# Storing the split weights of a four-chunk decoder block, a fifth place for them, and gates of 64 rows

## The chip, the core and the metric

One core of a Trainium2 chip runs the kernel in one launch. The metric is the device time of an execution in microseconds. The core's engines run beside each other and each takes its own instructions in order: TensorE (PE) multiplies, VectorE (DVE) and ScalarE (ACT) do element-wise work, SyncE (SP) issues nearly all DMA transfers, GpSimd (POOL) has almost nothing here. A DMA that SP issues may wait for a semaphore first; what is behind it in SP's program waits with it.

## What is computed

A decoder block of width 1024 over 2048 positions with 16 learned ones in front, in fp32. Cut to what matters:

```python
u = rmsnorm(h, mix_norm_g)
p = u @ w_in                                  # "W": 1024 x 1792
y = concat(pool(p_a), conformer(p_b), rglru(p_c))
h = h + y @ w_out                             # "O": 1024 x 1024
u = rmsnorm(h, mlp_norm_g)
h = h + square(relu(u @ w_up)) @ w_down       # "U" 1024 x 4096, "D" 4096 x 1024
out = rmsnorm(h, final_norm_g)[:, 16:]
# in rglru: 8 heads of 64 channels, two gates
r = sigmoid(einsum("bthc,hcd->bthd", xh, w_a) + b_a)
i = sigmoid(einsum("bthc,hcd->bthd", xh, w_x) + b_x)
```

## The kernel before

**Arithmetic.** Each fp32 operand of a product is held as a pair hi and lo: `split` (L109 to L111) rounds the source to hi with an ACT copy (L110) and takes lo as the rest with a DVE subtraction (L111). A product is three matmuls, hi·hi, hi·lo and lo·hi (`PRODS`), added in a PSUM bank.

**Tiling.** Channels lie on the 128 partitions, positions along the free axis, in four chunks of 512 columns; chunk 0 has the 16 learned positions besides, and its subtiles outside of O, U and D are 264 columns wide. A weight tile of 128x512 holds four 128-channel blocks of the contraction for one block of 128 output channels. For W, O and D an output tile (`mm_tile`) takes two weight tiles, each in 12 matmuls of 512 columns (L278; D's first two tiles of a group are interleaved, L292). In chunks 1 to 3 the up product U is a Strassen-Winograd scheme: 16 units of seven weight tiles, each tile in 12 matmuls of 256 columns (`up_unit`, L302). Of the seven, three are plain weights and four are sums and differences of weights, which chunk 0 works out (`gen_sums`) and leaves in the DRAM tensor `sums`.

**Order of the items.** W for chunks 0 and 1 interleaved, O for chunk 0, the rest of W for chunk 1; then for each chunk four groups of U and D. Behind the last D of chunk 0 stand O of chunk 1 and W of chunk 2, behind that of chunk 1 O of chunk 2 and W of chunk 3; O of chunk 3 stands within the last D group of chunk 2. O(c) and W(c) below are these products for chunk c, with tiles 0 to 7 of O and 0 to 13 of W.

**Weights.** The class `Weights` is one stream over all weight tiles in the order of use. `dma` loads a raw tile of 256 KB into one of six places `wr` (L141, on SP). `split` turns it into a tile `wh` of hi and lo, 128x1024, of which there are `WH` = 4 places; it does so under `tc.high_priority(EARLY)`, so the scheduler puts the two split instructions ahead of other work. A raw load waits until the split (L111) of an earlier tile has freed its place; a split waits until PE has read the `wh` tile that was in its place.

**Around O.** While PE runs O(c), ACT and DVE do two other things that load rows of the input through the two places `xr`. The evacuation `evac_o` of tile j loads the residual (L713), adds it to the PSUM tile into `h` (L715) and sums the squares of h (L345, L346). PE can't start a tile before the add of four tiles earlier has freed its PSUM bank (`pm` has four). And `gen_x` for chunk c+1 loads its eight input blocks (L412), sums their squares (L345, L346) and makes the pairs `U` that W will read (L148, L149). Both end in a `colsum` (L327, L328), two matmuls with a matrix of ones over the summed squares, then a square root (L335) and a reciprocal (L337). The scheduler lays the instructions of each engine in one list; waits and order are fixed when the program is built.

**Gates.** `gen_rg` takes a 128-channel block, that is two heads. `c_gw` holds block-diagonal 128x128 matrices, so each gate is three matmuls of 128 rows (`mm3`, L311 to L313) into a bank of `pb` (two banks) and one sigmoid of 128 partitions (L580).

## Time and profile before

| | |
|---|---|
| median of 3 runs | 1967.27 us (1966.43 to 1970.16) |
| the profiled execution | 1964.15 us, of which the span is 1962.2 us; granted clock 0.998 |
| PE busy | 1932.9 us, 99% of the span |
| DVE, ACT busy | 1508.6 us (77%), 1097.9 us (56%) |
| moved by DMA | 285.07 MB, 145 GB/s in the mean |

In the profile an instruction is named by its line, engine, operation and the tiles it writes and reads. "Idle before" is the time in which the engine stood before an instruction of the group, with what ended it. A row of the timeline gives the start, the length, and with "x24" a run of 24 like instructions; on SPq the length is that of issuing the transfers. The matmul's end is modelled: a matmul of 512 columns shows some 395 ns from start to end, but in a run of them the next starts long before that.

### The profile page before, as it was taken

Reading aid. Unit: us, or ns where it says so; the run is one execution under the profiler, and the core shown is the slowest. Engines: PE = TensorE matmul, PEld = TensorE weight load, DVE = VectorE, ACT = ScalarE, POOL = GpSimd, SP = SyncE. Lnnn points to the kernel's source line nnn. Section 1 sums busy time; section 2 is a strip of 40 time slices with the busy share of each in tenths; the row PEclk is TensorE's granted clock in tenths of the full one; section 3 lists DMA queues with packets and bytes.
Section 4 is the critical chain, followed back from the end, with each engine's and each line's share of the span. In section 5 each row is a group of like instructions: output and inputs, shape, how many; then the busy total and the mean of one; then the engine's idle time right before and its main releaser. Section 6 shows DMA issues by size and latency. Waiting matters only on the chain.

```text
span 1962.2 us, 29710 instructions
## 1 busy us (share of the span) xinstructions
PE 1932.9 (99%) x10648; PEld 1664.7 (85%) x10648; DVE 1508.6 (77%) x2419; ACT 1097.9 (56%) x1837; POOL 0.2 (0%) x4
## 2 busy tenths in 40 slices
PE   8999999999999999999999999999999999999998
PEld 8888878878888789898898778988989889889897
DVE  7986689977756899985776799986768597656477
ACT  6575463646544536675575453775658356445374
POOL 0000000000000000000000000000000000000000
PEclk9999999999999999999999999999999999999999
DMA  6412456645755435353444543544435434545354
GB/s 199 135 44 76 129 169 218 212 159 171 267 174 162 144 92 168 90 166 108 146 133 125 184 127 108 151 115 141 139 117 163 132 103 151 170 137 151 113 173 150
DMA packets 160035, 285.07 MB, mean 145 GB/s; under 512 B 17552, under 2 KB 23824, under 8 KB 159888
## 3 DMA queue, kind: packets, MB, share of 16 engines
q1 hardware_dynamic: 158304, 281.55, 46.6%
q8 instruction: 83, 1.36, 0.3%
q10 hardware_dynamic: 1584, 1.64, 0.2%
q14 instruction: 64, 0.52, 0.1%
HBM read 255.85 MB, written 27.26 MB: 144 GB/s over the span
## 4 chain that ended last, share of the span: by engine, by line
PE 77%; DVE 11%; DMA 6%; issue 3%; ACT 3%; SPq 1%; ACTq 0%; DVEq 0%
PE pm L278 47%; PE pm L302 11%; PE pw L302 9%; PE pm L292 7%; DVE wh L111 3%; DMA s<-d_w_up 2%; DMA xr<-d_xr 2%; DVE ca L535 1%; DMA t<-d_w_up 1%; DVE t L569 1%; DVE fr L821 1%; ACT wh L110 1%; DVE U L795 0%; DMA sums<-s 0%; PE pb L311 0%
## 5 line engine op out<-in xcount | busy, mean ns | idle before, releaser
L110 ACT ACTIVATE wh<-wr 128x512 fp32r<-128x512 f32 x828 | 517.1, 627 | 710.4 <-PE pm L278 482.9
L278 PE MATMUL pm<-U,wh 128*128 128x512 f32 (+1 forms) x3504 | 788.2, 384 | 0.6 <-DVE wh L111 0.6
L278 PEld LDWEIGHTS pm<-U,wh 128*128 128x128 f32 x3504 | 635.2, 188 | 141.0 <-DVE wh L111 1.0
L111 DVE TENSOR_TENSOR wh<-wr,wh 128x512 fp32r<-128x512 f32 x828 | 567.4, 689 | 208.6 <-ACT wh L110 204.1
L278 PE MATMUL pm<-H,wh 128*128 128x512 f32 (+1 forms) x2112 | 450.2, 372 | 8.0 <-ACT wh L110 6.5
L278 PEld LDWEIGHTS pm<-H,wh 128*128 128x128 f32 x2112 | 370.6, 190 | 82.9 <-ACT wh L110 6.5
L302 PE MATMUL pm<-H,wh 128*128 128x256 f32 x2304 | 292.5, 282 | 2.3 <-DVE wh L111 1.4
L302 PEld LDWEIGHTS pm<-H,wh 128*128 128x128 f32 x2304 | 282.3, 188 | 5.2 <-DVE wh L111 2.2
L302 PE MATMUL pw<-H,wh 128*128 128x256 f32 x1728 | 223.2, 282 | 1.6 <-DVE fr L821 1.6
L302 PEld LDWEIGHTS pw<-H,wh 128*128 128x128 f32 x1728 | 212.0, 189 | 4.6 <-DVE fr L821 3.9
L292 PE MATMUL pm<-U,wh 128*128 128x512 f32 (+1 forms) x768 | 176.1, 388 | 0.0
L292 PEld LDWEIGHTS pm<-U,wh 128*128 128x128 f32 x768 | 140.2, 188 | 30.9 <-DVE U L795 0.2
L535 DVE SCALAR_TENSOR_TENSOR ca<-Pbv,vec,ca 128x512 f32<-128x512 f32 x180 | 128.1, 748 | 0.0
L850 DVE TENSOR_TENSOR h<-h,pm 128x512 f32<-128x512 f32 (+1 forms) x106 | 71.6, 675 | 60.5 <-PE pm L278 45.6
L795 DVE TENSOR_TENSOR U<-fr,U 128x512 fp32r<-128x512 f32 x128 | 87.6, 687 | 11.4 <-ACT fr L794 11.4
L793 ACT ACTIVATE U<-fr 128x512 fp32r<-128x512 f32 x128 | 79.6, 624 | 1.9
L794 ACT ACTIVATE fr<-fr 128x512 f32<-128x512 f32 x128 | 79.3, 622 | 1.1
L821 DVE TENSOR_TENSOR fr<-pw,fr 128x512 f32<-128x512 f32 x96 | 66.1, 689 | 4.5 <-PE pw L302 1.9
L346 DVE TENSOR_TENSOR ss<-ss,fr 128x512 f32<-128x512 f32 (+1 forms) x82 | 53.3, 650 | 15.9 <-ACT fr L345 15.3
L337 DVE RECIPROCAL rs<-rs 128x512 f32<-128x512 f32 (+2 forms) x17 | 53.9, 3169 | 10.8 <-ACT rs L335 10.6
L535 DVE SCALAR_TENSOR_TENSOR ca<-h,vec,ca 128x512 f32<-128x512 f32 x60 | 42.8, 748 | 0.1
L841 ACT ACTIVATE fr<-fr 128x512 f32<-128x512 f32 x48 | 30.0, 625 | 12.1 <-DVE fr L840 11.8
(211 smaller groups left out, 1153.0 us busy)
## 6 DMA issues: line engine op xcount, KB each, us to landing
wr<-d_w_down SPq DMA_DIRECT2D x272, 256.0 KB, 2.9
wr<-d_w_up SPq DMA_DIRECT2D x208, 256.0 KB, 2.9
wr<-sums SPq DMA_DIRECT2D x192, 256.0 KB, 3.3
wr<-d_w_in SPq DMA_DIRECT2D x90, 256.0 KB, 2.7
xr<-d_xr SPq DMA_DIRECT2D x56, 256.0 KB, 2.8
wr<-wo_fold SPq DMA_DIRECT2D x32, 256.0 KB, 2.6
wr<-d_w_out SPq DMA_DIRECT2D x32, 256.0 KB, 2.6
s<-d_w_up SPq DMA_DIRECT2D x32, 256.0 KB, 3.8
```

The lines of the kernel that those rows point to most:

```text
L110: A.activation(out=hi, in_=src, func=AF.Copy)
L111: V.tensor_tensor(out=lo, in0=src, in1=hi.bitcast(F32), op=ALU.subtract)
L278: T.matmul(ps[:, : s1 - s0], w[k // 4][:, a, (k % 4) * P : (k % 4 + 1) * P], rhs[k][:, b, s0:s1], start=(k == 0 and j == 0), stop=(k == KB ...
L292: T.matmul(ps[:, : s1 - s0], w[k // 4][:, a, (k % 4) * P : (k % 4 + 1) * P], rhs[k][:, b, s0:s1], start=(k == 0 and j == 0), stop=(k == KB ...
L302: T.matmul(ps, w[:, a, k * P : (k + 1) * P], op[k // 2][:, b, (k % 2) * 256 : (k % 2) * 256 + 256], start=(k == 0 and j == 0), stop=(k == ...
L337: V.reciprocal(rs[:, c0:c1], rs[:, c0:c1])
L535: V.scalar_tensor_tensor(out=a, in0=o.ub[i][:, k : k + NT], scalar=vc("cw", i * CONVK + k), in1=a, op0=ALU.mult, op1=ALU.add)
L793: A.activation(out=f[:, 0], in_=r, func=AF.Square)
L794: A.activation(out=r, in_=r, func=AF.Square)
L795: V.tensor_tensor(out=f[:, 1], in0=r, in1=f[:, 0].bitcast(F32), op=ALU.subtract)
L821: V.tensor_tensor(out=out.rearrange("p (a c) -> p a c", a=2), in0=ps.rearrange("p (a c) -> p a c", a=2), in1=x.unsqueeze(1).broadcast_to([ ...
L850: V.tensor_tensor(out=h, in0=h, in1=ps[:, : s1 - s0], op=ALU.add)
```

## The change

Each split weight tile of W, of O and of the four sums of a U unit is written to DRAM once and loaded again as a pair. New DRAM tensors `w_kept` (28 tiles), `o_kept` (16) and `u_kept` (64), 512 KB each, take the `wh` tile behind its first split: W and O in the first use (28 and 16 stores), the sums in chunk 1 (64 stores). Where a tile has been kept, `split` issues one DMA from it into `wh` on SP (L271 in the new numbering), within the same `tc.high_priority(EARLY)`, in place of the raw load, the ACT copy and the DVE subtraction: 64 loads for W(2), W(3) and what W(1) takes again, 48 for O(1) to O(3), 128 for the sums in chunks 2 and 3. `WH` goes from 4 to 5, and with it the lookahead of the stream. In the gates `c_gw` becomes 128x512: rows 0 to 63 hold the even head's matrices, rows 64 to 127 the odd head's. A gate pair is now six matmuls of 64 rows each, alternating between the low and the high half and between two banks, and four sigmoids of 64 partitions (120 such matmuls in 25 runs over the program; before, 120 matmuls of 128 rows).

```diff
@@ -43,7 +43,7 @@
 HB = 14
 NU = D * 4 // (2 * P)
 WR = 6
-WH = 4
+WH = 5
 FR = 4
 LA_SPLIT = WH
 EARLY = 200
...
@@ -133,6 +133,9 @@
     cst = {}
 
     wo_fold = dp.tile([KB, P, 512], F32, name="wo_fold", tag="wo_fold")
+    w_kept = [[dp.tile([P, 2, 512], F32, name=f"wk_{b}_{q}", tag=f"wk_{b}_{q}") for q in range(2)] for b in range(14)]
+    o_kept = [[dp.tile([P, 2, 512], F32, name=f"ok_{j}_{q}", tag=f"ok_{j}_{q}") for q in range(2)] for j in range(KB)]
+    u_kept = [[dp.tile([P, 2, 512], F32, name=f"uk_{u}_{q}", tag=f"uk_{u}_{q}") for q in range(4)] for u in range(NU)]
     sums = [dp.tile([P, 2048], F32, name=f"sums_{u}", tag=f"sums_{u}") for u in range(NU)]
 
     def w_raw(src, tag="xr", bufs=2, queue=nc.sync):
...
@@ -205,9 +208,8 @@
         yield 1400
 
     def load_consts():
-        hl = t_("c_gw", (2, 1024), 1, F32R)
-        for c0 in (0, 512):
-            split(hl[:, 0, c0 : c0 + 512], hl[:, 1, c0 : c0 + 512], w_raw(gates[:, c0 : c0 + 512]))
+        hl = t_("c_gw", (2, 512), 1, F32R)
+        split(hl[:, 0], hl[:, 1], w_raw(gates))
         cst["gw"] = hl
         yield 1500
 
...
@@ -242,6 +244,8 @@
 
 
     class Weights:
+
+
         def __init__(self, srcs):
             self.srcs = srcs
             self.raw = {}
...
@@ -251,15 +255,24 @@
 
         def dma(self, n):
             while self.nd < min(n, len(self.srcs)):
-                self.raw[self.nd] = w_raw(self.srcs[self.nd](), "wr", WR, nc.sync if self.nd > 1 else nc.scalar)
+                if self.srcs[self.nd][2] is not None:
+                    self.nd += 1
+                    continue
+                self.raw[self.nd] = w_raw(self.srcs[self.nd][0](), "wr", WR, nc.sync if self.nd > 1 else nc.scalar)
                 self.nd += 1
 
         def split(self, n):
             while self.ns < min(n, len(self.srcs)):
                 self.dma(self.ns + 1)
                 t = t_("wh", (2, 512), WH, F32R)
+                _, keep, kept = self.srcs[self.ns]
                 with tc.high_priority(EARLY):
-                    split(t[:, 0], t[:, 1], self.raw.pop(self.ns))
+                    if kept is not None:
+                        nc.sync.dma_start(out=t.bitcast(F32), in_=kept)
+                    else:
+                        split(t[:, 0], t[:, 1], self.raw.pop(self.ns))
+                if keep is not None:
+                    nc.sync.dma_start(out=keep, in_=t.bitcast(F32))
                 self.hl[self.ns] = t
                 self.ns += 1
 
...
@@ -572,12 +585,18 @@
         w = cst["gw"]
         r = t_("t", W0, TB)
         g = t_("t", W0, TB)
-        for q, (dst, bias) in enumerate(((r, "ba"), (g, "bx"))):
-            for s0, s1 in subs_of(o):
-                ps = ps_back()
-                o_ = q * 512 + i * P
-                mm3(ps[:, : s1 - s0], [(w[:, 0, o_ : o_ + P], w[:, 1, o_ : o_ + P], hi[:, s0:s1], lo[:, s0:s1])])
-                A.activation(out=dst[:, s0:s1], in_=ps[:, : s1 - s0], func=AF.Sigmoid, bias=vc(bias, i))
+
+        low, high = slice(0, 64), slice(64, P)
+        for s0, s1 in subs_of(o):
+            n = s1 - s0
+            pa, pb_ = ps_back(), ps_back()
+            for j, (a, b) in enumerate(PRODS):
+                for ps, h in ((pa, low), (pb_, high)):
+                    T.matmul(ps[:, :n], w[h, a, i * P : (i + 1) * P], (hi, lo)[b][h, s0:s1], start=(j == 0), stop=(j == 2))
+            for dst, ps, to, of, bias in (
+                (r, pa, low, low, "ba"), (r, pb_, high, high, "ba"), (g, pa, low, high, "bxs"), (g, pb_, high, low, "bxs"),
+            ):
+                A.activation(out=dst[to, s0:s1], in_=ps[of, :n], func=AF.Sigmoid, bias=vc(bias, i)[of])
         yield 620
         csp = cst["csp"]
         a = t_("t", W0, TB)
...
@@ -951,31 +970,42 @@
         kind, c, j, _ = it
         if kind == "U" and c:
             m1, m2, s = w_up[2 * j], w_up[2 * j + 1], sums[j]
-            aps = (
-                (m1, 0), (m1, 512), (s, 0), (s, 1536), (s, 1024), (s, 512), (m2, 512),
-            )
-            return ("U", j), [lambda a=a, c0=c0: a[:, c0 : c0 + 512] for a, c0 in aps]
+            aps = [(m1, 0), (m1, 512), (s, 0), (s, 1536), (s, 1024), (s, 512), (m2, 512)]
+            r = []
+            for a, c0 in aps:
+                kept = u_kept[j][c0 // 512] if a is s else None
+                if kept is not None and c > 1:
+                    r.append((None, None, kept))
+                else:
+                    r.append((lambda a=a, c0=c0: a[:, c0 : c0 + 512], kept, None))
+            return r
+        keep = (None, None)
         if kind == "W":
-            a = w_in[_WORDER[j][2]]
+            b = _WORDER[j][2]
+            if c > 1 or ("W", b) in seen:
+                return [(None, None, t) for t in w_kept[b]]
+            a, keep = w_in[b], w_kept[b]
         elif kind == "U":
             a = w_up[j]
         elif kind == "D":
             a = w_down[j // KB, j % KB]
         else:
-            return ("O", j), [lambda: wo_fold[j], lambda: w_out[j]]
-        return (kind, a.offset if hasattr(a, "offset") else j, j), [lambda a=a, c0=c0: a[:, c0 : c0 + 512] for c0 in (0, 512)]
-
-    srcs, windex, last = [], [], None
+            if c:
+                return [(None, None, t) for t in o_kept[j]]
+            return [(lambda: wo_fold[j], o_kept[j][0], None), (lambda: w_out[j], o_kept[j][1], None)]
+        return [(lambda a=a, c0=c0: a[:, c0 : c0 + 512], keep[c0 // 512], None) for c0 in (0, 512)]
+
+    srcs, windex, last, seen = [], [], None, set()
     for it in items:
-        key, aps = sources(it)
-        if it[0] == "U":
-            key = ("U", it[1] > 0, it[2])
-        if it[0] == "W":
-            key = ("W", _WORDER[it[2]][2])
+        kind, c, j, _ = it
+        key = (kind, j if kind != "W" else _WORDER[j][2])
+        if kind == "U":
+            key += (c,)
         if key != last:
             first = len(srcs)
-            srcs.extend(aps)
+            srcs.extend(sources(it))
             last = key
+            seen.add(key)
         windex.append(first)
     wts = Weights(srcs)
 
...
@@ -1091,13 +1121,16 @@
...
-        "bx": _chan(a["rg_b_x"][0]), "rcb": _chan(a["rg_conv_b"][0]), "cb": _chan(a["convb_dw_b"][0]),
+        "bxs": np.roll(_chan(a["rg_b_x"][0]), 64, axis=0), "rcb": _chan(a["rg_conv_b"][0]), "cb": _chan(a["convb_dw_b"][0]),
...
-    gates = np.concatenate([_blockdiag(a["rg_w_a"][0]), _blockdiag(a["rg_w_x"][0])], axis=1).reshape(P, 1024)
+    gates = np.concatenate([
+        np.concatenate([a["rg_w_a"][0][0::2], a["rg_w_x"][0][0::2]], axis=2),
+        np.concatenate([a["rg_w_x"][0][1::2], a["rg_w_a"][0][1::2]], axis=2),
+    ], axis=1).transpose(1, 0, 2).reshape(P, 512)
```

**SP in O(2).** Before, from the second block of `gen_x`'s loads that are still out to the residual of tile 3: `wr` are raw weight loads, `xr` at L412 the input blocks for chunk 3, `xr_1758` and `xr_1778` at L713 the residuals of tiles 2 and 3.

```order
L412 DMA xr_1751_10348<-d_xr 128x512 [waits DMAHW5_49,DMAHW3_49,DVE_49]
L713 DMA xr_1758_10390<-d_xr 128x512 [waits DMAHW6_49,DMAHW4_49,DVE_49]
L141 DMA wr_1787_10488<-d_w_in 128x512 [waits DVE_49]
L141 DMA wr_1794_10528<-d_w_in 128x512 [waits DVE_49]
L412 DMA xr_1762_10398<-d_xr 128x512 [waits DMAHW7_49,DMAHW3_49,DVE_49]
L412 DMA xr_1765_10406<-d_xr 128x512 [waits DMAHW4_49,DMAHW0_49,DVE_49]
L141 DMA wr_1795_10530<-d_w_in 128x512 [waits DMAHW1_49,DVE_49]
L412 DMA xr_1768_10414<-d_xr 128x512 [waits DMAHW7_49,DMAHW2_49,DVE_49]
L141 DMA wr_1802_10570<-d_w_in 128x512 [waits DVE_49]
L412 DMA xr_1771_10422<-d_xr 128x512 [waits DMAHW0_49,DVE_49]
L141 DMA wr_1803_10572<-d_w_in 128x512 [waits DMAHW5_49,DVE_49]
L713 DMA xr_1778_10464<-d_xr 128x512 [waits DMAHW6_49,DMAHW2_49,DVE_49]
```

Now, the same place (L425 is L412 of before, L732 is L713): `wh` are loads of kept pairs, each waiting for PE; `ok_7_0` and `ok_7_1` are the two weight tiles of O's tile 7, `wk_2_0`, `wk_2_1` and `wk_4_0` the first ones of W(3); `xr_1692` and `xr_1710` are the residuals of tiles 2 and 3.

```order
L425 DMA xr_1684_10400<-d_xr 128x512 [waits DMAHW1_49,DVE_49]
L271 DMA wh_1728_10600<-ok_7_1_119 128x1024 [waits DMAHW2_49,PE_49]
L425 DMA xr_1687_10408<-d_xr 128x512 [waits DMAHW7_49,DMAHW3_49,DVE_49]
L271 DMA wh_1729_10602<-wk_2_0_80 128x1024 [waits DMAHW4_49,PE_49]
L732 DMA xr_1692_10444<-d_xr 128x512 [waits DMAHW5_49,DMAHW1_49,DVE_49]
L425 DMA xr_1696_10452<-d_xr 128x512 [waits DMAHW6_49,DMAHW3_49,DVE_49]
L425 DMA xr_1699_10460<-d_xr 128x512 [waits DMAHW5_49,DVE_49]
L425 DMA xr_1702_10468<-d_xr 128x512 [waits DMAHW6_49,DMAHW0_49,DVE_49]
L425 DMA xr_1705_10476<-d_xr 128x512 [waits DMAHW7_49,DVE_49]
L271 DMA wh_1734_10636<-wk_2_1_81 128x1024 [waits DMAHW2_49,PE_49]
L271 DMA wh_1735_10638<-wk_4_0_84 128x1024 [waits PE_49]
L732 DMA xr_1710_10512<-d_xr 128x512 [waits DMAHW4_49,DMAHW0_49,DVE_49]
```

The loads of `xr` stood between raw loads that waited for DVE; they now stand behind loads that wait for PE to be done with the weight tile five places back: for `wh_1728` the first half of tile 5, for `wh_1729` its second half, for `wh_1734` and `wh_1735` the two halves of tile 6.

**DVE at the end of O(2).** Before: `hl_1781` is the low half for the column sum, `h_1779` tile 3, `h_1790` tile 4.

```order
L346 TENSOR_TENSOR ss_1741_10324<-ss_1741_10324,fr_1772_10424 128x512 [waits DVE_49,Activation_49]
L149 SCALAR_TENSOR_TENSOR U_1770_10421<-xr_1771_10422,vec_1_69,U_1770_10421 128x512 [waits DMAHW4_49,Activation_49]
L111 TENSOR_TENSOR hl_1781_10471<-ss_1741_10324,hl_1781_10471 128x512 [waits Activation_49]
L715 TENSOR_TENSOR h_1779_10466<-pm_1777_10439,xr_1778_10464 128x512 [waits DMAHW6_49]
L111 TENSOR_TENSOR wh_1809_10609<-wr_1787_10488,wh_1809_10609 128x512 [waits DMAHW5_49,Activation_49]
L337 RECIPROCAL rs_1783_10477<-rs_1783_10477 128x512 [waits Activation_49]
L111 TENSOR_TENSOR wh_1835_10681<-wr_1794_10528,wh_1835_10681 128x512 [waits Activation_49]
L346 TENSOR_TENSOR ss_1730_10260<-ss_1730_10260,fr_1780_10468 128x512
L715 TENSOR_TENSOR h_1790_10517<-pm_1788_10490,xr_1789_10515 128x512 [waits DMAHW0_49]
```

Now: `hl_1713` is that low half, `h_1711` tile 3, `h_1720` tile 4 (L734 is L715 of before, L350 is L337).

```order
L359 TENSOR_TENSOR ss_1677_10384<-ss_1677_10384,fr_1706_10478 128x512 [waits DVE_49,Activation_49]
L152 SCALAR_TENSOR_TENSOR U_1704_10475<-xr_1705_10476,vec_1_69,U_1704_10475 128x512 [waits DMAHW1_49,Activation_49]
L111 TENSOR_TENSOR hl_1713_10519<-ss_1677_10384,hl_1713_10519 128x512 [waits Activation_49]
L350 RECIPROCAL rs_1715_10525<-rs_1715_10525 128x512 [waits Activation_49]
L734 TENSOR_TENSOR h_1711_10514<-pm_1709_10487,xr_1710_10512 128x512 [waits DMAHW4_49,PE_49]
L734 TENSOR_TENSOR h_1720_10559<-pm_1718_10532,xr_1719_10557 128x512 [waits DMAHW5_49,PE_49]
L359 TENSOR_TENSOR ss_1668_10326<-ss_1668_10326,fr_1712_10516 128x512 [waits Activation_49]
L359 TENSOR_TENSOR ss_1668_10326<-ss_1668_10326,fr_1721_10561 128x512 [waits DVE_49,Activation_49]
```

The add of tile 3 stood ahead of the reciprocal and now stands behind it.

**PE in the gates of chunk 1.** Before, one block's two gates, with the matmuls of W around them:

```order
L278 MATMUL pm_508_2969<-U_466_2740,wh_500_2922 128x512 x3
L311 MATMUL pb_512_3000<-hl_509_2995,c_gw_97_504 128x512
L312 MATMUL pb_512_3000<-hl_509_2995,c_gw_97_504 128x512 [waits DVE_49]
L313 MATMUL pb_512_3000<-hl_509_2995,c_gw_97_504 128x512
L311 MATMUL pb_513_3005<-hl_509_2995,c_gw_97_504 128x512
L312 MATMUL pb_513_3005<-hl_509_2995,c_gw_97_504 128x512
L313 MATMUL pb_513_3005<-hl_509_2995,c_gw_97_504 128x512
L278 MATMUL pm_519_3028<-U_395_2360,wh_504_2959 128x512 [waits Activation_49]
```

Now (L595 is the new matmul, L291 is L278 of before):

```order
L291 MATMUL pm_501_3114<-U_459_2885,wh_492_3064 128x512 x3
L595 MATMUL pb_505_3145<-hl_502_3140,c_gw_99_628 128x512
L595 MATMUL pb_506_3146<-hl_502_3140,c_gw_99_628 128x512
L595 MATMUL pb_505_3145<-hl_502_3140,c_gw_99_628 128x512 [waits DVE_49]
L595 MATMUL pb_506_3146<-hl_502_3140,c_gw_99_628 128x512
L595 MATMUL pb_505_3145<-hl_502_3140,c_gw_99_628 128x512
L595 MATMUL pb_506_3146<-hl_502_3140,c_gw_99_628 128x512
L291 MATMUL pm_512_3175<-U_388_2505,wh_493_3067 128x512 [waits Activation_49]
```

Six matmuls in three and three became six in alternation between two banks; their number is the same.

More of the change, by code (lines that the diff above doesn't have):

```diff
@@ L60 @@
 _VECS = [
-    ("g1", 8), ("g2", 8), ("gf", 8), ("psc", 2), ("lam", 4), ("ba", 4), ("bx", 4),
+    ("g1", 8), ("g2", 8), ("gf", 8), ("psc", 2), ("lam", 4), ("ba", 4), ("bxs", 4),
     ("rcb", 4), ("cb", 2), ("lng", 2), ("lnb", 2), ("rcw", 16), ("cw", 62),
@@ L1112 @@
     "x0": (KB, P, W0), "xr": (NCH - 1, KB, P, NT), "w_in": (14, P, D), "w_out": (KB, P, 512), "w_fold": (4, P, D), "w_up": (32, P, D),
-    "w_down": (FG, KB, P, D), "vecs": (P, NVEC), "gates": (P, 1024), "pools": (P, 256), "pws": (P, 512),
+    "w_down": (FG, KB, P, D), "vecs": (P, NVEC), "gates": (P, 512), "pools": (P, 256), "pws": (P, 512),
 }
```

## The prediction

> **What bounds the kernel.** I read the busy times first, then the busy time in six stretches, then the waits of PE.
>
> ```profile
> PE 1932.9 (99%) x10648; PEld 1664.7 (85%) x10648; DVE 1508.6 (77%) x2419; ACT 1097.9 (56%) x1837; POOL 0.2 (0%) x4
> 0.00:130.00 130.00, 120.75 (x741) 107.78 (x742) 115.91 (x226) 83.21 (x126) 0.20 (x4) 1.00 0.43 136
> 130.00:600.00 470.00, 467.08 (x2015) 376.42 (x2013) 352.08 (x547) 257.76 (x417) 0.00 (x0) 1.00 0.53 168
> 600.00:1100.00 500.00, 495.12 (x2764) 428.08 (x2763) 395.41 (x627) 285.36 (x477) 0.00 (x0) 1.00 0.44 133
> 1100.00:1200.00 100.00, 98.70 (x420) 78.37 (x420) 90.42 (x146) 49.90 (x83) 0.00 (x0) 1.00 0.48 152
> 1200.00:1600.00 400.00, 398.82 (x2363) 351.33 (x2362) 308.49 (x484) 235.34 (x398) 0.00 (x0) 1.00 0.44 132
> 1600.00:1962.00 362.00, 352.45 (x2353) 322.67 (x2351) 246.31 (x394) 186.36 (x336) 0.00 (x0) 0.99 0.49 148
> PE pm L278 <- ACT wh L110: 6.5, 1, 6.5
> 1953.30 0.70 PE L865 MATMUL pb<-fr,ones 128*128 128x256 f32 x2 [0.59 <-ACT fr L856]
> ```
>
> A stretch's row gives its length, then PE, PEld, DVE, ACT and POOL busy, the granted clock, the share of DMA time and GB/s. PE is idle for 9.2, 2.9, 4.9, 1.3, 1.2 and 9.6 us, 29.1 in all. The first wait of the program is 6.5 of them, and 8.2 lie behind the last matmul, which ends at 1954.0 of 1962.2. **So some 14 us are all that a better supply of weights can win**; the rest is PE's own work. That work is paced by the start of the next matmul:
>
> ```profile
> 632.64 15.95 PE L278 MATMUL pm<-H,wh 128*128 128x512 f32 x68
> 844.58 3.03 PE L302 MATMUL pm<-H,wh 128*128 128x256 f32 x24
> L278 PE MATMUL pm<-H,wh 128*128 128x512 f32 x1632 | 384.1, 395 | 0.8 <-DVE h L715 0.5 <-DVE wh L111 0.2
> ```
>
> 68 matmuls of 512 columns take 15.95 us with the last one's 0.395: 0.232 us apart. 24 of 256 columns, by the same reckoning with 0.28, 0.119 apart. A weight tile of W, O or D is 12 x 0.232 = 2.8 us of PE, an O tile 5.6; a U tile 1.43, a unit of seven 10.0.
>
> **What the change takes away.**
>
> ```profile
> L110 ACT ACTIVATE wh<-wr 128x512 fp32r<-128x512 f32 x828 | 517.1, 627 | 710.4 <-PE pm L278 482.9
> L111 DVE TENSOR_TENSOR wh<-wr,wh 128x512 fp32r<-128x512 f32 x828 | 567.4, 689 | 208.6 <-ACT wh L110 204.1
> SPq L141 <- DVE wh L111: 1276.6, 741, 10.1
> ```
>
> 240 splits go: 240 x 0.627 = 150 us of ACT and 240 x 0.689 = 165 us of DVE. All of it ran beside PE: ACT's copies waited 483 us for PE, so they were early. It gains nothing beyond the 14 us. The third row is the side effect: SP's raw loads waited for the DVE split, 741 times. A kept load waits for PE instead, since it writes the `wh` place itself, and everything behind it on SP waits too. The two lists of SP's order show what that is in O(2): the residuals and the input blocks in `xr`.
>
> **O(2), step by step.** What one `xr` place costs is read from the same stage of before:
>
> ```profile
> 1121.99 0.33 SPq L412 DMA_DIRECT2D xr<-d_xr  x1
> 1124.65 0.63 ACT L345 ACTIVATE fr<-xr 128x512 f32<-128x512 f32 x1 [1.30 <-DMA xr<-d_xr]
> 1125.94 0.75 DVE L149 SCALAR_TENSOR_TENSOR U<-xr,vec,U 128x512 fp32r<-128x512 f32 x1
> 1126.72 0.33 SPq L713 DMA_DIRECT2D xr<-d_xr  x1
> 1126.78 0.63 ACT L345 ACTIVATE fr<-xr 128x512 f32<-128x512 f32 x1 [0.36 <-DMA xr<-d_xr]
> 1128.86 0.49 PE L327 MATMUL pb<-hl,ones 128*128 128x512 f32 x1 [0.97 <-ACT hl L110]
> 1129.45 0.68 DVE L715 TENSOR_TENSOR h<-pm,xr 128x512 f32<-128x512 f32 x1
> 1129.59 0.50 PE L328 MATMUL pb<-hl,ones 128*128 128x512 f32 x1 [0.23 <-DVE hl L111]
> 1130.19 5.85 PE L278 MATMUL pm<-H,wh 128*128 128x512 f32 x24
> 1130.85 3.35 DVE L337 RECIPROCAL rs<-rs 128x512 f32<-128x512 f32 x1
> ```
>
> Issue to landing 2.7 (1121.99 to 1124.65); a place used for an input block is free again after 4.7 (1126.69), one used for a residual after 3.4 (1126.72 to 1130.13). From the last block's square to the column sum 2.1 (1126.78 to 1128.86), its second half 0.7 later, the end of the reciprocal 4.6 behind that (1134.20). A kept load's issue: 0.45, that is 0.33 and my 0.1 for the wake.
>
> Let 0 be the end of tile 5. `wh_1722`, `wh_1723`, `wh_1728` and `wh_1729` go out when the halves of tiles 4 and 5 end (-8.4, -5.6, -2.8, 0, each plus 0.45), and behind each one `xr` load. One place: `xr_1681` at -7.9, `xr_1687` at -2.3, `xr_1696` at 2.4, `xr_1702` at 7.1. The other: `xr_1684` at -5.1, and the residual of tile 2, `xr_1692`, at 0.45; it lands at 3.2, its add ends at 3.9. Tile 6 needs that add's bank: **PE waits 3.9**. Tile 6 runs to 9.5. `xr_1699` goes out at 3.9, the last block `xr_1705` at 8.6; it lands at 11.3, and the column sum starts at 13.4: **3.9 more, and 0.5** for the second half at 14.1. Then DVE's list decides: the add of tile 3, for which tile 7 waits, now stands behind the reciprocal, which ends at 18.7; the add at 19.4: **5.1**. Together 13.4. The second column sum, one and a half tiles later, is in time by the same chain.
>
> **O(1)** has the same lists with tile 3's add ahead of the reciprocal. `xr_925` and `xr_930` stand behind the load that the end of tile 5's first half frees: tile 6 waits 2.5. The other blocks follow two by two, `xr_940` at 7.9, `xr_943` at 9.1, the column sum at 14.0: 5.9. The residual of tile 3 goes out at 12.6, its add ends at 16.0: 1.9, and 0.3 for the second half. Together 10.6.
>
> What these stages lose already:
>
> ```profile
> 649.00:660.00 11.00, 8.39 (x28) 6.35 (x29) 9.30 (x12) 4.14 (x8) 0.00 (x0) 0.84 0.44 129
> 1127.00:1137.00 10.00, 8.70 (x34) 6.04 (x33) 9.45 (x12) 4.90 (x9) 0.00 (x0) 1.00 0.49 158
> ```
>
> 28 matmuls are 6.5 us of work in 11: 4.5 lost, of which 2.6 idle and the rest the clock of 0.84 behind a wait of 1.8; 34 are 7.9 in 10: 2.1. Taking 1.8 for the clock after the last long wait of each stage in the new kernel: O(1) 10.6 + 1.8 - 4.5 = +7.9, O(2) 13.4 + 1.8 - 2.1 = +13.1. **+21.** Lower end: only the waits that the queue alone forces, a residual issued when its place's predecessor frees (0.45 + 2.7 + 0.7 = 3.9), twice in O(2), once in O(1): 7.8 - 2.1 + 3.9 - 4.5 = +5. Upper end: seven landings in series, at 3.8 us as the nearest loaded row below, +1.1 each: +29.
>
> **Gates.** PE issues 120 matmuls as before, in 60 pairs of a low and a high half.
>
> ```profile
> L312 PE MATMUL pb<-hl,c_gw 128*128 128x512 f32 x24 | 9.5, 396 | 0.0
> L312 PE MATMUL pb<-hl,c_gw 128*128 128x264 f32 x16 | 4.6, 297 | 0.4 <-DVE st L601 0.3
> L312 PEld LDWEIGHTS pb<-hl,c_gw 128*128 128x128 f32 x40 | 7.5, 188 | 2.6 <-DVE hl L111 1.3
> L580 ACT ACTIVATE t<-pb,vec 128x512 f32<-128x512 f32 x24 | 15.9, 686 | 0.3
> L580 ACT ACTIVATE t<-pb,vec 128x264 f32<-128x264 f32 x16 | 7.4, 479 | 7.9 <-PE pb L313 7.8
> ```
>
> No row shows two halves at once. If the halves of a pair run side by side, 36 pairs save 0.232 and 24 save 0.12 (by proportion): -11.2; if not, 0. At 50 changes between whole and half tiles the next matmul may have to wait for the end of the one before: 0.396 - 0.232 = 0.16 each, +8.2; with its weight load no longer hidden 0.188 more, +17.6. I take side by side with the first price, since every run of the rows overlaps its weight loads: **-3** (-11.2 to +6.4). The Trainium skill states both halves of it (TensorEngine Tiling (Array Packing), section Key Properties): tiles work in parallel, and changing the tiling mode drains the engine. No run here shows either yet. By its first rule alone the sum would be 8 lower, by the second alone 11 higher. The sigmoids double, +16 us on ACT by 24 x 0.686, +8 by 16 x 0.479; ACT is busy 56% and loses 150: 0.
>
> **Kept sums in U(2) and U(3).** A kept load goes out when the tile five back ends and is needed four tiles later, 5.7 us.
>
> ```profile
> wr<-d_w_up SPq DMA_DIRECT2D x208, 256.0 KB, 2.9
> s<-d_w_up SPq DMA_DIRECT2D x32, 256.0 KB, 3.8
> t<-d_w_up SPq DMA_DIRECT2D x32, 256.0 KB, 4.8
> q1 hardware_dynamic: 158304, 281.55, 46.6%
> ```
>
> 281.55 MB in 46.6% of 1962.2 us make 308 GB/s for busy engines. 512 KB: 2.9 + 0.85 for 256 KB more + 0.45 = 4.2, in time; from 4.8 instead of 2.9 it is 6.1, late by 0.4 in each of 32 units. I take **-1**: the idle of 1200 to 1600 and some of U(3)'s go; ends -2.5 and +13.
>
> **Stores in U(1).** A unit loads 7 x 256 KB and stores 4 x 512 KB, 3.93 MB; at 308 GB/s 12.8 us against PE's 10.0. Four units in a row lag 11 us; up to 11 tiles lie ahead of PE (6 raw, 5 split), 15.7 us less a landing of 2.9. Just covered: **0**, up to +19 at a tenth less rate (four groups, 4.8 each). The Trainium skill (DMA: Bandwidth & Descriptors, Specifications) gives some 358 GB/s as the memory limit of a core, below the 393 that PE's pace asks for; by it the lag is 1 us a unit, and the sum stays.
>
> **The rest**: the stores of W and O in chunk 0 lie in 290 us of PE work; the fifth place and the early waits of 130 to 600: **-1** (-5 to +3). The head and the tail stay.
>
> **Sum**: 1964.15 + 21 - 3 - 1 - 1 = 1980 for the profiled execution, whose own time lies 3.1 below the median of the runs; **1983** for the median.
>
> **Rivals.** *The gates' halves run side by side without a price* (the faster side). It decides if the O stages cost under 11: with their lower end, 1967 + 5 - 11 - 4 = 1957. For it: no drain is seen in any row. Against: the lists fix the order, and the lower end leaves out that two places serve 13 loads. *The DMA engines fill in U(1)*: 1983 + 15 = 1998. For it: 393 GB/s asked, 267 the busiest slice; against: the prefetch.
>
> ```profile
> GB/s 199 135 44 76 129 169 218 212 159 171 267 174 162 144 92 168 90 166 108 146 133 125 184 127 108 151 115 141 139 117 163 132 103 151 170 137 151 113 173 150
> ```
>
> *Each change of tile size costs the exposed weight load too*: gates +6, 1992. *Nothing changes*: O's waits come out near their lower end and the gates and U pay for them: 1967.
>
> **Chances.** Forecast 0.55, full DMA 0.15, dear gates 0.10, no change 0.09, faster 0.11. A measurement of this kernel can tell about 0.2%, that is 1963.3 to 1971.2, from no change. Slower 0.80, same 0.09, faster 0.11. The range 1964 to 2003 leaves out the faster case and the ends of the DMA one.
>
> **What would show it.** In the new profile: tile 6 of O(1) and O(2) with PE idle 2 to 4 us before it, released by DVE's `h` (L734); before the column sums 4 to 6; before tile 7 of O(2) 5, behind the reciprocal; `wh` loads waiting for PE on SPq right ahead of `xr`; gate pairs starting together or 0.23 apart; U(1) without PE waits on raw splits, DMA above 300 GB/s there. I am wrong if O's idle stays under 8 us in all, or if the `xr` loads go out earlier than the halves of tiles 4 to 6 end.

## The result, and the profile after

| | before | changed |
|---|---|---|
| median of 4 runs each | 1966.85 us (1965.01 to 1970.16) | 1996.61 us (1994.55 to 1999.27) |
| ratio, with its 95% interval | | 1.015 (1.0132 to 1.0168) |
| span of the profiled execution | 1962.2 us | 1994.5 us |

The changed kernel is slower by 30 us; the prediction was slower by 16, with 1983 us and a range of 1964 to 2003. First its page (totals, the transfers and the two split groups) and then its waits, of PE and of SP's queue (us in total, times, longest):

```profile
PE 1938.9 (97%) x10648; PEld 1659.4 (83%) x10648; DVE 1363.8 (68%) x2178; ACT 981.0 (49%) x1630; POOL 0.2 (0%) x4
q1 hardware_dynamic: 173712, 400.83, 60.7%
L110 ACT ACTIVATE wh<-wr 128x512 fp32r<-128x512 f32 x588 | 366.0, 627 | 557.0 <-PE pm L291 368.5
L111 DVE TENSOR_TENSOR wh<-wr,wh 128x512 fp32r<-128x512 f32 x588 | 401.8, 688 | 208.6 <-ACT wh L110 194.6
...
PE pm L291 <- DVE h L734: 15.5, 3, 5.9
PE pb L340 <- ACT hl L110: 8.5, 3, 6.2
PE pw L315 <- DVE fr L840: 7.8, 12, 1.5
...
SPq L144 <- DVE wh L111: 724.3, 404, 5.8
SPq L271 <- PE pm L291: 268.3, 128, 7.3
```

The 240 splits are gone as planned, 151 us of ACT and 166 of DVE, and the kernel is slower: that work lay beside PE. In return 119 MB more are moved, SP's queue waits for PE (L271, a new row), and PE waits for the residual add `h` (0.5 us in the kernel before, 15.5 now), for the column sums (4.2 and 8.5) and in U for `fr` (1.6 and 7.8), the place into which DVE empties a PSUM tile of U (L840).

Where the time went is read by setting marks that both kernels have, in chunk 0 and again in chunk 1: the start of the pair of tiles of the last D group (L292, now L305) and the first matmul of the next U (L302, now L315). Timeline rows of before, then of the changed kernel:

```profile
564.21 4.11 PE L292 MATMUL pm<-U,wh 128*128 128x512 f32 x17
738.24 4.45 PE L302 MATMUL pm<-H,wh 128*128 128x256 f32 x36
1041.64 1.10 PE L292 MATMUL pm<-U,wh 128*128 128x512 f32 x4
1044.21 2.02 PE L292 MATMUL pm<-U,wh 128*128 128x512 f32 x8
1215.08 4.44 PE L302 MATMUL pm<-H,wh 128*128 128x256 f32 x36
```

```profile
565.19 7.13 PE L305 MATMUL pm<-U,wh 128*128 128x512 f32 x30
750.68 4.48 PE L315 MATMUL pm<-H,wh 128*128 128x256 f32 x36
1059.19 2.03 PE L305 MATMUL pm<-U,wh 128*128 128x512 f32 x8
1245.81 4.44 PE L315 MATMUL pm<-H,wh 128*128 128x256 f32 x36
```

At the third mark the orders differ: in the kernel before, four of the pair's 48 matmuls stand ahead of U's last 12, and the other 44 start at 1044.21. For the same work on both sides its third mark is set four matmuls earlier, at 1044.21 - 4 x 0.232 = 1043.28.

From the first to the second mark lie the end of chunk 0, O(1) and W(2): 174.0 before, 185.5 now. From the third to the fourth, with O(2) and W(3): 171.8 and 186.6. From second to third, U and D of chunk 1: 305.0 and 308.5. So of 32.3 us of span 11.5 and 14.8 come from the two O stretches; 3.5 from chunk 1, and the remaining 2.6 from the start and from all behind the fourth mark.

What O(2) looks like now, from the end of tile 5 on (timeline; PE works on tile 5 until 1137.9):

```profile
1137.95 0.32 SPq L271 DMA_DIRECT2D wh<-wk  x1
1138.91 0.33 SPq L732 DMA_DIRECT2D xr<-d_xr  x1
1143.07 0.69 DVE L734 TENSOR_TENSOR h<-pm,xr 128x512 f32<-128x512 f32 x1 [1.11 <-DMA xr<-d_xr]
1143.82 8.54 PE L291 MATMUL pm<-H,wh 128*128 128x512 f32 x24 [5.90 <-DVE h L734]
1153.25 0.50 PE L340 MATMUL pb<-hl,ones 128*128 128x512 f32 x1 [0.89 <-ACT hl L110]
1155.23 3.35 DVE L350 RECIPROCAL rs<-rs 128x512 f32<-128x512 f32 x1 [1.31 <-ACT rs L348]
1158.50 1.22 DVE L734 TENSOR_TENSOR h<-pm,xr 128x512 f32<-128x512 f32 x2
1159.19 7.07 PE L291 MATMUL pm<-H,wh 128*128 128x512 f32 x21 [4.71 <-DVE h L734]
```

The residual of tile 2 is issued behind the kept load that the end of tile 5 frees, its add starts 4.2 us later, and tile 6 starts 5.9 us late. Then its 24 matmuls take 8.54 us instead of 5.7: PE runs at half its pace after the wait. Tile 7 waits for an add that stands behind the reciprocal, 4.7. The two O stages as stretches of 36 us, with PE busy (the first number behind the comma) and the granted clock (the third from the right):

```profile
636.00:672.00 36.00, 24.88 (x85) 19.09 (x84) 18.18 (x24) 12.06 (x20) 0.00 (x0) 0.81 0.60 197
1130.00:1166.00 36.00, 24.27 (x82) 18.39 (x81) 20.29 (x26) 13.05 (x21) 0.00 (x0) 0.81 0.63 207
```

85 and 82 matmuls are 19.7 and 19.0 us of work: 16.3 and 17.0 are lost, of which 11.1 and 11.7 idle and 5.2 and 5.3 by the clock. The half pace comes twice in each stage: in O(1) the granted clock is 0.50 in these two stretches, in O(2) from 1142.95 and from 1156.60 on, each time for 6.8 us.

```profile
648.02:654.84 6.82, 5.92 (x14) 4.67 (x15) 4.72 (x8) 3.00 (x5) 0.00 (x0) 0.50 0.36 121
661.67:668.49 6.82, 4.82 (x11) 3.62 (x12) 5.31 (x7) 3.75 (x6) 0.00 (x0) 0.50 0.38 123
```

### The profile page after: what moved, and what is told of

It reads as the page before. It is cut to its first block, busy times and chain, and to the rows that moved or that the text cites. A ratio compares the mean times of both kernels' runs of the same rounds, so it can differ in the third digit from the quotient of the medians.

```text
span 1994.5 us, 29086 instructions
## 1 busy us (share of the span) xinstructions
PE 1938.9 (97%) x10648; PEld 1659.4 (83%) x10648; DVE 1363.8 (68%) x2178; ACT 981.0 (49%) x1630; POOL 0.2 (0%) x4
## 4 chain that ended last, share of the span: by engine, by line
PE 81%; DMA 7%; DVE 6%; ACT 3%; issue 2%; SPq 0%; ACTq 0%; DVEq 0%
PE pm L291 53%; PE pm L315 9%; PE pm L305 9%; PE pw L315 8%; DMA xr<-d_xr 2%; DVE wh L111 2%; DMA uk<-wh 1%; DMA wr<-d_w_in 1%; DMA wh<-uk 1%; ACT wh L110 1%; DVE ca L548 1%; PE pb L595 1%; DVE fr L840 1%; DMA s<-d_w_up 1%; ACT t L599 1%
## 5 line engine op out<-in xcount | busy, mean ns | idle before, releaser
L291 PE MATMUL pm<-U,wh 128*128 128x512 f32 (+1 forms) x3504 | 790.2, 384 | 0.3 <-DVE U L152 0.3
L291 PEld LDWEIGHTS pm<-U,wh 128*128 128x128 f32 x3504 | 634.5, 188 | 144.0 <-issue 1.6
L110 ACT ACTIVATE wh<-wr 128x512 fp32r<-128x512 f32 x588 | 366.0, 627 | 557.0 <-PE pm L291 368.5
L111 DVE TENSOR_TENSOR wh<-wr,wh 128x512 fp32r<-128x512 f32 x588 | 401.8, 688 | 208.6 <-ACT wh L110 194.6
L291 PE MATMUL pm<-H,wh 128*128 128x512 f32 (+1 forms) x2112 | 457.6, 376 | 24.7 <-DVE h L734 15.5
L291 PEld LDWEIGHTS pm<-H,wh 128*128 128x128 f32 x2112 | 374.9, 192 | 103.0 <-DVE h L734 17.0
L315 PE MATMUL pm<-H,wh 128*128 128x256 f32 x2304 | 290.5, 282 | 0.0
L315 PEld LDWEIGHTS pm<-H,wh 128*128 128x128 f32 x2304 | 281.1, 188 | 2.6 <-ACT wh L110 0.7
L315 PE MATMUL pw<-H,wh 128*128 128x256 f32 x1728 | 224.1, 283 | 9.9 <-DVE fr L840 7.8
L315 PEld LDWEIGHTS pw<-H,wh 128*128 128x128 f32 x1728 | 212.4, 189 | 14.0 <-DVE fr L840 8.0
L305 PE MATMUL pm<-U,wh 128*128 128x512 f32 (+1 forms) x768 | 176.0, 388 | 0.0
L305 PEld LDWEIGHTS pm<-U,wh 128*128 128x128 f32 x768 | 140.4, 188 | 31.0
L840 DVE TENSOR_TENSOR fr<-pw,fr 128x512 f32<-128x512 f32 x96 | 66.1, 688 | 27.2 <-PE pw L315 25.2
L358 ACT ACTIVATE fr<-h 128x512 f32<-128x512 f32 (+1 forms) x45 | 27.8, 621 | 76.2 <-DVE h L734 49.0
L350 DVE RECIPROCAL rs<-rs 128x512 f32<-128x512 f32 (+2 forms) x17 | 53.9, 3168 | 12.7 <-ACT rs L348 12.6
```

The costliest lines, as they stand in the source:

```text
L110: A.activation(out=hi, in_=src, func=AF.Copy)
L111: V.tensor_tensor(out=lo, in0=src, in1=hi.bitcast(F32), op=ALU.subtract)
L291: T.matmul(ps[:, : s1 - s0], w[k // 4][:, a, (k % 4) * P : (k % 4 + 1) * P], rhs[k][:, b, s0:s1], start=(k == 0 and j == 0), stop=(k == KB ...
L305: T.matmul(ps[:, : s1 - s0], w[k // 4][:, a, (k % 4) * P : (k % 4 + 1) * P], rhs[k][:, b, s0:s1], start=(k == 0 and j == 0), stop=(k == KB ...
L315: T.matmul(ps, w[:, a, k * P : (k + 1) * P], op[k // 2][:, b, (k % 2) * 256 : (k % 2) * 256 + 256], start=(k == 0 and j == 0), stop=(k == ...
L350: V.reciprocal(rs[:, c0:c1], rs[:, c0:c1])
```

## The experiments

Each kernel is the changed one with the edit shown, but for the last; two build on the run with `xr` on ACT's queue. The stretches are measured between the marks above in the profiled execution. Over before means above 174.0 and 171.8. (In the last run the orders at the third mark are those of the kernel before, and the mark is set in the same way. Forecasts that name 15.8 or 7.0 us for O(2) had before's mark at 1044.21; they are 0.9 high.)

| run | median, us | ratio to before (95%) | O(1), W(2) | O(2), W(3) | chunk 1 |
|---|---|---|---|---|---|
| before | 1967 | | 174.0 | 171.8 | 305.0 |
| changed | 1996.6 | 1.015 (1.0132 to 1.0168) | 185.5 | 186.6 | 308.5 |
| xr on GpSimd's queue | 1987.7 | 1.0105 (1.009 to 1.012) | 183.3 | 181.9 | 308.4 |
| W, O raw | 1974.3 | 1.004 (1.0026 to 1.0055) | 174.2 | 172.0 | 310.1 |
| sums raw | 1987.5 | 1.0106 (1.0091 to 1.0121) | 183.9 | 186.8 | 304.1 |
| gates alone | 1968.6 | 1.001 (0.9999 to 1.002) | 172.5 | 171.2 | 305.7 |
| kept W, O on GpSimd's queue | 1989.9 | 1.0118 (1.0097 to 1.0139) | 181.2 | 180.9 | 308.9 |
| xr on ACT's queue | 1983.4 | 1.0083 (1.0066 to 1.0101) | 178.7 | 177.9 | 308.7 |
| O raw | 1976.1 | 1.005 (1.0034 to 1.0066) | 176.1 | 174.7 | 307.6 |
| three xr places | 1980.3 | 1.0067 (1.0051 to 1.0083) | 174.7 | 178.7 | 307.8 |
| xr on ACT's queue, half the bytes | 1975.7 | 1.0045 (1.0028 to 1.0062) | 173.1 | 175.1 | 308.0 |
| xr on ACT's queue, three places | 1983.2 | 1.0072 (1.0052 to 1.0093) | 177.1 | 178.2 | 308.2 |
| gates, three places, nothing kept | 1965.4 | 0.9983 (0.9974 to 0.9992) | 171.2 | 171.4 | 304.9 |
| before, three places | 1959.8 | 0.9962 (0.9949 to 0.9976) | 170.9 | 170.8 | 304.5 |

**One part at a time.** First, which part costs what.

```diff
-            if c > 1 or ("W", b) in seen:
-                return [(None, None, t) for t in w_kept[b]]
-            a, keep = w_in[b], w_kept[b]
+            a = w_in[b]
...
-            if c:
-                return [(None, None, t) for t in o_kept[j]]
-            return [(lambda: wo_fold[j], o_kept[j][0], None), (lambda: w_out[j], o_kept[j][1], None)]
+            return [(lambda: wo_fold[j], None, None), (lambda: w_out[j], None, None)]
```

> The changed kernel without kept W and O: their tiles are loaded raw and split each time, as before; the sums stay kept, WH stays 5, the gates stay. Theory: kept W and O cost the two O stretches, 11.5 and 15.8 us; the median is near 1969 (1966 to 1973), what is left being U's extra stalls less the gates' gain. Rival: the fifth place or the high priority of the sums' loads also delays O, then one of the two stretches keeps 4 us or more and the median is above 1976.

```diff
-                kept = u_kept[j][c0 // 512] if a is s else None
+                kept = None
```

> The changed kernel without kept sums: no stores in chunk 1, and chunks 2 and 3 load the raw sums and split them, as before; W and O stay kept. Theory: the stores delay raw loads in U(1), 5 us of PE waits there, and the kept loads cost 1 to 2 us in U(2) and U(3): median near 1991 (1988 to 1993), with O(1) and O(2) as in the changed kernel. Rival: U's waits come from the order of DVE and ACT with a fifth place and stay: 1996.

With W and O raw both stretches are back to 0.2 over before: kept W and O cost 25.9 of the 26.3 us. With raw sums chunk 1 takes 4.4 less than in the changed kernel and the median falls by 9.1, where some 5.6 were expected; the O stretches stay. The median of the run with raw W and O lies above its forecast for the same reason: U costs more than I allowed. How U(1) loses it, in the changed kernel (a window of it, a row of ACT's waits, and one such wait in the timeline):

```profile
744.00:784.00 40.00, 38.84 (x297) 37.26 (x296) 38.56 (x63) 20.86 (x39) 0.00 (x0) 1.00 0.87 304
ACT wh L110 <- DMA uk<-wh: 12.7, 9, 2.5
860.34 0.63 ACT L110 ACTIVATE wh<-wr 128x512 fp32r<-128x512 f32 x1 [1.23 <-DMA uk<-wh]
861.62 0.68 DVE L840 TENSOR_TENSOR fr<-pw,fr 128x512 f32<-128x512 f32 x1
862.36 1.68 PE L315 MATMUL pw<-H,wh 128*128 128x256 f32 x12 [1.04 <-DVE fr L840]
```

304 GB/s with the engines busy 87% of the time (177 and 58% in the kernel before, over 738 to 778); with raw sums PE is busy all 40 us of the same window. The second row is a wait that the prediction didn't name: a stored tile's place is free only when its store has read it, not when PE has, so the next split waits, DVE's list behind it, and PE for `fr` (6.4 of its 7.8 us lie in chunk 1; with raw sums 2.2 are left there).

Both edits together, and four places again:

```diff
-WH = 5
+WH = 4
```

> The kernel before with the new gates alone (nothing kept, WH 4). Theory: a run of six matmuls with its two changes of tile size takes 1.22 instead of 1.64 us, 0.42 saved in ten to twelve runs of chunks 1 to 3, nothing in chunk 0's short runs: 1962.5 (1961 to 1964.5). Rival: sigmoids of half the partitions and waits for two banks give it back: 1967.

A run of six: before and changed, timeline of PE.

```profile
789.70 0.40 PE L311 MATMUL pb<-hl,c_gw 128*128 128x512 f32 x1
791.09 1.09 PE L278 MATMUL pm<-U,wh 128*128 128x512 f32 x4
```

```profile
803.55 0.96 PE L595 MATMUL pb<-hl,c_gw 64*128 64x512 f32 x6
804.44 1.90 PE L291 MATMUL pm<-U,wh 128*128 128x512 f32 x7
```

From the first gate matmul to the next whole one 1.39 us became 0.89, and the entry costs 0.1 more: the halves of a pair start together, 3 to 7 ns apart in the trace, and each run saves 0.41. But the kernel isn't faster: it comes to the first mark 2.9 us later (567.1 against 564.2), though four of the runs of six lie ahead of it. The scheduler laid DVE's list in chunk 0 anew, and there two splits stand behind adds of `gen_sums` that wait for their loads, with PE waiting 1.7 and 1.2 us (timeline of the run with the gates alone, the first of them):

```profile
544.50 0.69 DVE L200 TENSOR_TENSOR t<-s,t 128x512 f32<-128x512 f32 x1 [4.34 <-DMA s<-d_w_up]
545.83 0.68 DVE L111 TENSOR_TENSOR wh<-wr,wh 128x512 fp32r<-128x512 f32 x1
546.57 8.59 PE L291 MATMUL pm<-H,wh 128*128 128x512 f32 x36 [1.74 <-DVE wh L111]
```

**Order or traffic.** Both theories say that `xr` is late in O. In one it leaves late, behind kept loads that wait for PE; in the other it lands late, beside 512 KB transfers.

```diff
-            nc.sync.dma_start(out=raw, in_=xr[o.c - 1, k])
+            (nc.gpsimd if o.c > 1 else nc.sync).dma_start(out=raw, in_=xr[o.c - 1, k])
```

(and the same in `evac_o` for chunks 1 and 2; 32 transfers in all)

> The changed kernel with one edit: the input blocks and residuals (xr) that O(1) and O(2) load are issued on GpSimd's queue instead of SP's, 34 transfers; the kept loads stay on SP. Theory 'order': these loads were late because they stood behind kept loads that wait for PE; then the stretches from the last D group of chunks 0 and 1 to the first U of the next chunk shorten by about 10 and 14 us, PE no longer waits for h (L734) over 1 us in tiles 6 and 7, and the median is near 1972 (1967 to 1977). Rival 'traffic': they were late because 512 KB loads fill the engines; then the landings of xr stay at 3.5 to 5.8 us, the waits stay above half, and the median is above 1984.

9.3 and 10.1 over before, the rival's numbers. The waits on tiles 6 went, those on the column sums grew to 11.9 and 9.7. But on this queue a landing took 4.4 us in the median, against 3.4 on SP in the changed kernel, and whether that is the queue or the traffic this run can't tell.

Now the other way round, the kept loads of W and O on GpSimd's queue (`pool` is set for these) and `xr` on SP:

```diff
-                        nc.sync.dma_start(out=t.bitcast(F32), in_=kept)
+                        (nc.sync if pool is None else nc.gpsimd).dma_start(out=t.bitcast(F32), in_=kept)
```

> The changed kernel with the kept loads of W and O issued on GpSimd's queue; xr stays on SP, where now nothing waits for PE in O. Theory 'order': xr goes out as early as its two places allow; the stretches from the last D group to the next U cost 0 to 3 us over before each (11.5 and 15.8 in the changed kernel), median 1970 to 1977. Rival 'traffic' (as the first try with xr on GpSimd's queue suggests, where landings took 4.4 us in the median): 512 KB loads lengthen xr's landing on any queue, two places then serve a block each 3 us instead of 2.4, and the stretches keep 6 us or more each, median above 1982.

In O nothing on SP waits for PE now, and still the stretches keep 7.2 and 9.1: the rival's numbers again.

Then `xr` on ACT's queue, where a landing took 3.3 us in the median:

```diff
-            nc.sync.dma_start(out=raw, in_=xr[o.c - 1, k])
+            (nc.scalar if o.c > 1 else nc.sync).dma_start(out=raw, in_=xr[o.c - 1, k])
```

> The changed kernel with the xr loads of O(1) and O(2) issued on ACT's queue, kept loads on SP. 'Order': landings near 3 us, stretches 0 to 3 us over before, median 1970 to 1977. 'Traffic': landings of 4 us and more, stretches 6 us or more over before, median above 1982, much like the try with GpSimd's queue (1988).

4.7 and 6.1 over before, between the two forecasts and nearer to that of traffic. Taking `xr` out of SP's order is worth 15.5 of the 26.3 us, and 10.8 stay with `xr` on a queue of its own. Not all of the 15.5 is the queue: DVE's list was laid anew too. In O(2) the add of tile 3 stands ahead of the reciprocal again so the wait of 4.7 us for tile 7 went with DVE's order:

```profile
1142.30 0.69 DVE L734 TENSOR_TENSOR h<-pm,xr 128x512 f32<-128x512 f32 x1 [0.80 <-DMA xr<-d_xr]
1143.67 3.35 DVE L350 RECIPROCAL rs<-rs 128x512 f32<-128x512 f32 x1 [0.67 <-ACT rs L348]
```

The next run builds on this one and halves the bytes: of the kept tiles of W(2), W(3), O(1) and O(2) only the high half is loaded, and the third product reads it in place of the low one, so the low halves of these weights are left out of the result. PE's and DVE's lists stay as they are; on SP some output stores move ahead of a kept load.

```diff
-                        nc.sync.dma_start(out=t.bitcast(F32), in_=kept)
+                        nc.sync.dma_start(out=t[:, 0].bitcast(F32), in_=kept[:, 0])
```

> The run with xr on ACT's queue (1983.4, stretches 4.6 and 7.0 us over before) with one difference: a kept tile of W(2), W(3) and of O(1), O(2) is loaded as its high half alone, 256 KB, and the third product reads the high half again, so the low halves of these weights are left out of the result. Every engine's order is the same, only the bytes are halved. 'Traffic': xr lands in about 3 us, the stretches fall to 0 to 2 us over before, median 1972 to 1976. Rival 'ACT': what was left came from loads waiting their turn among ACT's instructions; the stretches stay, median 1982 to 1985.

The stretches fall to -0.9 and 3.3, by 8.4 together: traffic. The same part of O(2), the 22 us from 56.1 us behind the third mark on, in the two runs and in the one with three places on ACT's queue below, by the stretch view; the last two numbers are the busy share of the DMA engines and GB/s. The fourth row is 5 us of the third. Then the landings of the six `xr` loads that are issued in the last 19 us, with whole pairs and with half the bytes:

```profile
1108.00:1130.00 22.00, 22.00 (x97) 17.86 (x96) 10.11 (x16) 6.26 (x10) 0.00 (x0) 1.00 0.99 346
1102.63:1124.63 22.00, 22.00 (x97) 17.77 (x96) 10.38 (x17) 7.16 (x12) 0.00 (x0) 1.00 0.82 277
1109.33:1131.33 22.00, 18.96 (x82) 15.04 (x81) 11.43 (x19) 7.44 (x13) 0.00 (x0) 1.00 0.99 362
1114.00:1119.00 5.00, 5.00 (x23) 4.06 (x22) 2.65 (x4) 2.08 (x4) 0.00 (x0) 1.00 1.04 403
...
xr<-d_xr ACTq DMA_DIRECT2D x6, 256.0 KB, 5.4
xr<-d_xr ACTq DMA_DIRECT2D x6, 256.0 KB, 3.8
```

With whole pairs the engines are full, 346 GB/s; O needs the pair, `xr` and the chunk's output stores at once. With half the bytes they are busy 0.82 of the time, and `xr` lands 1.6 us sooner. The Trainium skill (DMA: Bandwidth & Descriptors, Specifications) puts a core's memory limit at some 358 GB/s. The third row, 362 over 22 us, is close to it, but the fourth has 403 over 5 us, so here that figure is no limit.

```diff
-            raw = t_("xr", NT, 2)
+            raw = t_("xr", NT, 3)
```

(and so for every user of the tag), once with all loads on SP,

> The changed kernel with three xr places instead of two. A residual or block can be asked for one step earlier, so tile 2's residual stands behind the load that tile 4 frees and no longer behind the one that tile 5 frees. 'Order' and places together: tile 6 waits 0 to 1, the column sum 1 to 2, tile 7 about 2 us, stretches 2 to 6 us over before each, median about 1977. If the DMA engines are the limit a third place adds nothing: above 1990.

and once with `xr` on ACT's queue:

> The run with xr on ACT's queue, and three xr places instead of two, the kept loads whole. If slow landings cost through the two places, a third covers a landing of up to 6 us: stretches 0 to 2 us over before, median 1972 to 1976. If the engines are full, no place helps: 1981 or more.

On SP a third place is worth 18.7 of the 26.3: the scheduler asks for tile 2's residual a step earlier, in O(2) 74.2 us behind the third mark instead of 79.7. O(1) keeps 0.7 and O(2) 6.9, below and above the 2 to 6 that were expected for each. Beside `xr` on ACT's queue it is worth 1.3, where 10 were expected: with the engines full (the third row above) the rival's forecast holds, and in that run the places weren't the limit.

Of the first edit only the part for O:

> The changed kernel with O loaded raw and split as before; W and the sums stay kept. 'Order': only the first W loads stand ahead of xr at the end of O, so tile 6 no longer waits and tile 7 does for about 3 us: stretches 3 to 6 us over before each, median about 1979. 'Traffic': O's bytes are halved but for the W loads at its end, so xr lands in 3 us and the stretches are 0 to 3 over before, median about 1973.

2.1 and 2.9 over before. Raw O takes away both its bytes and its waits on PE. Both numbers lie in the forecast of traffic, the second at the edge of that of order, and the median, 1976, halfway between the two: this run doesn't decide between them. What is left, some 5 us, goes with the kept W loads, since with W raw as well 0.4 remain.

**A faster kernel.** The kernel before has waits of its own in O(1) and O(2), and a third place had not been tried on it. First with the gates and nothing kept, then alone:

```diff
-            raw = t_("xr", NT, 2)
+            raw = t_("xr", NT, 3)
```

> Nothing kept, WH 4, the new gates and three xr places: a try for a kernel faster than both. The gates alone gave 1968.6 (their 0.42 us a run was given back in chunk 0); the third place takes away what O(1) and O(2) lose in the kernel before, 4.5 and 2.1 us. Median 1963 (1961 to 1966). Rival: the places were not what O(1) and O(2) of before waited for: 1968.

> The kernel before with three xr places and nothing else. The run with the new gates and three places was 0.17% under before, with one wait of 2.4 and one of 2.3 us left in O(1) and O(2). If the third place gives it, this is as fast: 1964 (1962 to 1966). If the gates give it (0.41 us a run of six in chunks 1 to 3, some 4 us, with chunk 0's loss gone), this is like before: 1967.

With this number changed the kernel before runs in 1959.8 us, 0.38% less (0.24 to 0.51%), its two stretches 3.1 and 1.0 shorter. It beats both kernels. With the gates beside it some 4 us of this are lost (ratios 0.9983 and 0.9962): that run comes to the first mark 6.1 us later than the kernel before.

## Why the prediction was right, and what it missed

*What bounds the kernel.* Right: PE's work, and 317 us less of ACT and DVE bought nothing.

*O(1) and O(2), +21.* Right in kind, place and sign. The idle time came out as worked out: 10.6 and 13.4 forecast, 11.1 and 11.7 measured. The parts differ: tile 6 waited 4.9 and 5.9 where 2.5 and 3.9 were forecast, since in O(2) the residual went out 1.0 us behind the end of tile 5 instead of 0.45 and took 4.2 us to the start of its add (1138.91 to 1143.07) instead of 2.7, and the first landings of O(1) took 5.9; the column sum of O(2) waited 0.9 instead of 3.9, partly because tile 6 ended so late; tile 7 4.7 instead of 5.1. **The term of O that was mis-sized is the clock.** I took 1.8 us for each stage, once, as O(1) of the kernel before loses behind its wait of 1.8. Now each stage has two stretches at half the clock, and they cost 5.2 and 5.3, that is 6.9 more than I took: 16.3 + 17.0 - 4.5 - 2.1 = 26.7 instead of 21.

*The cause* was half of it. The sum treated every late landing as late issue. Taking the order away, DVE's with SP's, leaves 10.8 of 26.3 us, and halving the bytes takes 8.4 of these: taken away in this sequence, order made some 15, traffic some 8, and 2.4 stay unassigned. The rival "the DMA engines fill" was placed in U(1), at 1998 us, and 1996.6 came out; but that is luck, since chunk 1 lost 3.5 us and not 15. Full engines were found in O(2), where I hadn't looked for them.

*Gates, -3.* Right for the term: 0.41 in each of ten runs (two more are broken up by other matmuls and save less), side by side, at 0.1 for each change of tile size instead of 0.16. By the rule of the Trainium skill that tiles work in parallel (TensorEngine Tiling (Array Packing), Key Properties) the trace agrees; of the drain it shows 0.1 us. Missed: the new list in chunk 0 takes 2.9 us net, and the run with the gates alone is no faster.

*Sums in U(2) and U(3), -1, and stores in U(1), 0.* Wrong in sign within their ranges. With raw sums chunk 1 is 4.4 shorter and what lies behind the fourth mark 3.5 (748.7 and 745.2). A kept sum's landing was 4.8 us in the median, where I had allowed 3.75, and in U(1) the place held by the store was left out:

```profile
wh<-uk SPq DMA_DIRECT2D x128, 512.0 KB, 4.8
uk<-wh SPq DMA_DIRECT2D x64, 512.0 KB, 4.5
wh<-ok SPq DMA_DIRECT2D x48, 512.0 KB, 4.2
xr<-d_xr SPq DMA_DIRECT2D x56, 256.0 KB, 3.4
```

*The rest, -1*: the stretch up to the first mark is 1.0 longer. *The sum*: the profiled execution took 1996.7 us, 16.5 more than the 1980 forecast. 5.3 of this is O (26.3 instead of 21), 8.9 the sums (7.9 by the run with raw sums, instead of -1), and the other 2.3 the gates and the rest. So the larger part of the miss lies in terms that were put at nothing or at a gain, and the range held because it was wide.

*The rivals.* Free gates: the gates ran side by side, but O cost 26, so it never decided. Dear gates: a change of tile size costs 0.1 us and not 0.35, so it is out. Nothing changes: excluded by the interval.

What stays open: 2.4 us of O behind the half-byte run, and how much of the 18.7 us that a third place saved on SP is order and how much is landings covered. With whole pairs and all loads on SP that run still took 3.2 us less in O than the one with `xr` on ACT's queue, so the split into order and traffic holds for the sequence of runs here and isn't a property of the bytes alone. How much of the 15.5 us that `xr` on ACT's queue saved is DVE's order alone was not run apart. The kernel with the gates alone gives back 6.0 us (4.1 saved in ten runs, yet the span is 1.9 longer); 4.5 of these lie ahead of the first mark, the rest is not found. A version with kept pairs whose loads are issued behind `xr` on the same queue was not tried.

## What to carry to other kernels

Work that an engine does beside the one that sets the time is worth nothing by its busy time; before it is traded for transfers, ask which queue they stand in, what each of them waits for, and whose data stands behind them. A load straight into its final place waits for the last reader, so it belongs on a queue where nothing else is urgent, and its bytes must fit beside what the same stage already moves: here another queue gave back 10 to 16 of 26 us, and half the bytes another 8. Where a chain through two buffers paces a stage, a third buffer is the cheapest thing to try first: here it alone beat both kernels.
